# A down projection by seven multiplications: where the sums of weights are made

## The chip, the cores and the metric

The kernel runs on one core of a Trainium2 chip. The metric is the device time of one launch in microseconds; the kernel before was timed three times. All numbers of the profile are of one profiled execution on that core.

## What is computed

One decoder block on 256 tokens and 16 meta tokens, width 2048, in float32: a norm and one wide input projection, an RWKV-7 branch and a forgetting-attention branch side by side, a gated merge, an output projection, and a SwiGLU feed-forward network. Its last line is the part that is changed:

```python
def _layer(h, n1, w_in, ..., n2, w_gu, w_dn):
    ...
    h = h + merged @ w_o
    gate, up = jnp.split(_rms(h, n2) @ w_gu, 2, axis=-1)
    return h + (jax.nn.silu(gate) * up) @ w_dn
```

`w_dn` is 5632 x 2048. The result is held to float32 accuracy: every operand is split into a high part `wh` (rounded by ACT) and the rest `wl` (the difference, by DVE), and a product is three matmuls, high by high, high by low and low by high.

## The kernel before

The kernel is one program for five engines: PE (matmuls), ACT, DVE, POOL, and SP, which issues most DMAs. Weights are streamed once. A *job* is a slab of weights: a `load` (SP's DMA into one of four `raw` buffers, ACT's split into one of four `wh` buffers, DVE's into one of four `wl` buffers) and a `mul` (the matmuls). `run` issues the load of a job ahead of the matmuls of the job before it, so that splits run ahead of PE, by up to four buffers. `spawn` starts side work that is let in between by an estimate of PE's time, here the sums of activations (`sums_of_pairs`).

The down projection takes `w_dn` in 22 *pairs* of 128 rows (256 rows each) and two *column groups* `cg` of 1024 columns, each of two halves of 512. The activations of a pair, already split, are in `ach` and `acl`, 128 tokens by 128 rows a block, two blocks of tokens `t`. So a pair and a column group is a 2x2 product of blocks: activations A (tokens by rows) times weights B, with blocks b11, b12 (first 128 rows, left and right half) and b21, b22 (second 128 rows). There are two ways to do it:

- *slow* pairs (15 of 22): eight products, in two plain jobs of four products each, one for each half of the columns;
- *fast* pairs (7 of 22, `FAST`): seven products by Winograd's form of Strassen's scheme, with sums of blocks of A (made once, into `sst` and over a block of `acl` and `ach`) and sums of blocks of B, made for each column group. Four products (p1, p5, p6, p7) are added up over all fast pairs in four PSUM tiles `dnp` (`ps` in the code); the other three go straight into the plain accumulators `dn` (`cs`). After the last fast pair `sums_of_products` adds p1, p5, p6, p7 into the residual `hh` with one ACT copy (`u`) and eight additions on DVE.

A fast pair's sums of weights before: `load0` fetches b11, b12 in one DMA of 512 KB and b21, b22 in two of 256 KB, into two `raw` buffers; `load2` makes four differences on DVE, b12 - b11, b22 - (b12 - b11), b22 - b12 and b21 - (b22 - (b12 - b11)), into two `tt` tiles; splits of the raw blocks and of the differences feed the products, as four small jobs.

`ORDER` fixes which pairs follow each other: in column group 0 eight slow pairs, then fast and slow in turn; in column group 1 slow, fast, slow, slow, fast, and so on, with two slow pairs after the last fast one. The order of instructions within an engine is then set by the framework's own scheduler; each engine runs its instructions in that order, and waits at semaphores. The tiles `hts` (activations of the up projection) and `sst` share one buffer of the pool `hp`.

Of the kernel before, what the change touches and what calls it, by code (L numbers as in the profile page):

```python
# [18 lines left out]
P = 128  # L19
# [3 lines left out]
T = 256  # L23
# [18 lines left out]
for _n, _k in (("n1", 16), ("mu", 24), ("mu_w", 1), ("mu_a", 1), ("mu_g", 2), ("w0", 8), ("a0", 8), ("k_k", 8),  # L42
# [22 lines left out]
MIX = 0.47  # L65


FAST = [0, 1, 2, 3, 4, 5, 6]
# [48 lines left out]
def hybrid_block(ctx, tc, A, out, dbg=None):  # L117
# [391 lines left out]
    def split(hi, lo_, src):  # L509
        nc.scalar.activation(hi, src, AF.Copy)  # L510
        nc.vector.tensor_tensor(lo_, src, hi.bitcast(F32), op=ALU.subtract)
# [789 lines left out]
    hp = hp_pool.__enter__()  # L1301
    hh = hp.tile([P, 2, D], F32, tag="hh", name="hh")

    hts = hp.tile([P, KT, 2, L], F32R, tag="hts", name="hts")
# [32 lines left out]
    for j in range(4):  # L1337
        js = slice(j * 512, (j + 1) * 512)
        nc.sync.dma_start(hh[:, :, js], x[:, js].rearrange("(t p) c -> p t c", p=P))

        def post(t, ps, j=j, js=js):
            nc.vector.tensor_tensor(hh[:, t, js], ps, hh[:, t, js], op=ALU.add)
            jk = hp.tile([P, 512], F32, tag="jk", name=f"jk{j}{t}", bufs=2)
            nc.scalar.activation(jk, hh[:, t, js], AF.Square, accum_out=ss2[:, t, j:j + 1])
            if t == 0:
                return
            for k in range(4 * j, 4 * j + 4):
                pt = aux_ps(f"hT{k}")[:, :T]
                for t in range(2):
                    nc.tensor.transpose(pt[:, t * P:(t + 1) * P], hh[:, t, k * P:(k + 1) * P], ident)  # L1350
                tmp = hp.tile([P, T], F32, tag="htmp", name=f"htmp{k}", bufs=3)
# [63 lines left out]
    sst = sst[:, :len(fast) * 6 * P].rearrange("p (i s a c) -> p i s a c", i=len(fast), s=3, a=2)  # L1415

    def sums_of_pairs():

        at = 0
        for n in BATCHES:  # L1420
            fs, ps_ = slice(at, at + n), slice(fast[at], fast[at] + n)
            at += n
            h = lambda k, t: acp_h[:, ps_, k, t, :].bitcast(F32)
            l = lambda k, t: acp_l[:, ps_, k, t, :].bitcast(F32)
            f = [sst[:, fs, i, 1, :] for i in range(3)] + [acp_l[:, ps_, 0, 1, :]]
            hi = [sst[:, fs, i, 0, :] for i in range(3)] + [acp_h[:, ps_, 0, 1, :]]
            f32 = [hp.tile([P, T], F32, tag="ga", name=f"s{at}{i}", bufs=8)[:, :n * P].rearrange("p (i c) -> p i c", c=P)
                   for i in range(4)]
# [5 lines left out]
            tt(0, f32[0], l(1, 1), ALU.add)  # L1434
# [5 lines left out]
            tt(3, h(1, 0), f32[1], ALU.subtract)  # L1440
# [13 lines left out]
    def rows(ap):  # L1454
        return ap.rearrange("p (r c) -> p r c", c=T)

    def product(ps, a, w, half, first, last):
        o = ps.rearrange("p (a c) -> p a c", a=2)
        hi, lo_ = (x_[:, 2 * half:2 * half + 2] for x_ in w)
        nc.tensor.matmul(o, a[0], hi, start=first, stop=False)  # L1460
        nc.tensor.matmul(o, a[1], hi, start=False, stop=False)  # L1461
        nc.tensor.matmul(o, a[0], lo_, start=False, stop=last)  # L1462
        slot(3 * 512 / 2.4)

    def split_tiles():
        return [wp.tile([P, WCOLS], F32R, tag=t, name=t, bufs=WB).rearrange("p (r c) -> p r c", c=L)[:, :, s:s + T]
                for t, s in zip(("wh", "wl"), PLACE_T)]
# [17 lines left out]
            return load, mul  # L1485
        return [mk(0), mk(1)]

    def fast_jobs(i, cg, cs, ps, end):
        box = {}

        def b(k, x_):
            return wdn[i * 256 + k * P:i * 256 + (k + 1) * P, cg * 1024 + x_ * 512:cg * 1024 + (x_ + 1) * 512]

        def load0():
            ra, rb = (wp.tile([P, 1024], F32, tag="raw", name="raw", bufs=RAWB) for _ in range(2))
            nc.sync.dma_start(ra, wdn[i * 256:i * 256 + P, cg * 1024:(cg + 1) * 1024])
            for x_ in range(2):
                nc.sync.dma_start(rb[:, (1 - x_) * 512:(2 - x_) * 512], b(1, x_))
            box["r"] = rows(ra), rows(rb)
            w = split_tiles()  # L1500
            split(*(t[:, 0:2] for t in w), box["r"][0][:, 0:2])
            return w

        def load1():
            w = split_tiles()
            split(*w, box["r"][1])
            return w

        def load2():
            (b11, b12), (b22, b21) = ([r[:, 0:2], r[:, 2:4]] for r in box["r"])  # L1510
            w, v = split_tiles(), split_tiles()
            ts = [rows(hp.tile([P, 1024], F32, tag="tt", name="tt", bufs=2)) for _ in range(2)]
            t1, t2, t3, t4 = (t[:, 2 * n:2 * n + 2] for t in ts for n in range(2))
            for o, x_, y_ in ((t1, b12, b11), (t2, b22, t1), (t3, b22, b12), (t4, b21, t2)):
                nc.vector.tensor_tensor(o, x_, y_, op=ALU.subtract)
            split(*w, ts[0])
            box["v"] = v, ts[1]
            return w

        def load3():  # L1520
            v, t = box["v"]
            split(*v, t)
            return v

        first = i == fast[0]

        def mul0(w):
            if not ps:
                ps.extend(aux_ps(f"dnp{cg}{n}") for n in range(4))
            product(ps[0], a_of(i, 0, 0), w, 0, first, end)  # L1530

        def mul1(w):
            product(cs[1], s_of(i, 3), w, 0, False, False)
            product(cs[0], a_of(i, 1, 0), w, 1, False, False)

        def mul2(w):
            product(ps[1], s_of(i, 0), w, 0, first, end)
            product(ps[2], s_of(i, 1), w, 1, first, end)

        def mul3(w):  # L1540
            product(ps[3], s_of(i, 2), w, 0, first, end)
            product(cs[2], a_of(i, 1, 1), w, 1, False, False)
            if end:
                sums_of_products(cg, ps)
        return [(load0, mul0), (load1, mul1), (load2, mul2), (load3, mul3)]

    def sums_of_products(cg, ps):
        p1, p5, p6, p7 = ps
        h11, h12, h21, h22 = (hh[:, t, (2 * cg + x_) * 512:(2 * cg + x_ + 1) * 512] for t in range(2) for x_ in range(2))
        u = hp.tile([P, 512], F32, tag="jk", name=f"u{cg}", bufs=2)  # L1550
        nc.scalar.activation(u, p1, AF.Copy)
        for o, x_ in ((u, p6), (h11, p1), (h12, p5), (h12, u), (u, p7), (h22, p5), (h21, u), (h22, u)):
            nc.vector.tensor_tensor(o, x_, o, op=ALU.add)

    def post(cg, t, x_, ps):

# [7 lines left out]
    spawn(sums_of_pairs(), 2 * PAIRS)  # L1564
    for cg in range(2):
        cs, ps = [], []
        for i in ORDER[cg]:
            if i in fast:
                run(fast_jobs(i, cg, cs, ps, i == fast[-1]))
            else:  # L1570
                run(slow_jobs(i, cg, cs, i == ORDER[cg][-1]))
    finish_job()
    hp_pool.__exit__(None, None, None)
    ap_pool.__exit__(None, None, None)

# [60 lines left out]
```

## Time and profile before

| | |
|---|---|
| time of three runs | 1520.84 us median (1520.27 to 1521.56) |
| span of the profiled execution | 1517.7 us (its own time is given by the span alone) |
| busy share of PE, DVE, ACT, POOL | 99%, 73%, 53%, 7% |
| instructions of PE, DVE, ACT, POOL | 10071, 2009, 1230, 182 |
| granted TensorE clock, mean | 1.000 |
| bytes moved | 283.32 MB, 187 GB/s in the mean |
| down projection | about 1281 to 1518 us of the span |

The span is from the first to the last instruction; the time of a run holds some work around it. A row of a group reads: line, engine, operation, out<-in by tile names, shapes, count | busy us, mean ns of one | idle time of the engine before it, and what ended it. A row of waits reads: waiting engine and line <- releasing engine and line: us in all, times, longest. `SPq` and the like are an engine's DMA queue; "to landing" is from the issue of a DMA to the end of its data.

### The profile page before, as it was taken

To read this page: it belongs to the slowest core of one execution; us is meant where nothing else is said; L and a number is where in the kernel's file an instruction comes from. 1 tells how busy PE (TensorE), PEld (TensorE's weight loads), DVE (VectorE), ACT (ScalarE), POOL (GpSimd) and SP (SyncE) were. 2 spreads that over 40 slices of the span, in tenths; PEclk is the share of its full clock that TensorE was granted. 3 is DMA by queue.
4 is the path that set the end of the run, shared out by engine and by line. 5 is a ranking of instruction groups with operands and counts; after the bars stand their busy time and mean duration, and the time that the engine had idled before them with its cause. 6 is when DMAs were issued, how large, how long until landed. Compare 5 with 4: busy or idle time off the path is not lost.

```text
span 1517.7 us, 26174 instructions
## 1 busy us (share of the span) xinstructions
PE 1509.9 (99%) x10071; PEld 1339.5 (88%) x10071; DVE 1112.0 (73%) x2009; ACT 808.3 (53%) x1230; POOL 99.3 (7%) x182
## 2 busy tenths in 40 slices
PE   9999999999999999999999999999999999999998
PEld 9999999999989888998888888888888888887887
DVE  7888699689789857875665666566566658879776
ACT  7664565475465545644554555454455545554543
POOL 2112202202202000000000000000000000000000
PEclk9999999999999999999999999999999999999999
DMA  8557456646645757777566666666666666566664
GB/s 271 166 166 212 119 156 185 170 122 173 188 127 149 223 152 214 234 231 240 181 179 192 189 187 193 191 186 192 190 187 191 193 186 182 178 211 201 213 206 138
DMA packets 210365, 283.32 MB, mean 187 GB/s; under 512 B 24320, under 2 KB 129296, under 8 KB 210240
## 3 DMA queue, kind: packets, MB, share of 16 engines
q1 hardware_dynamic: 205344, 277.25, 61.9%
q10 hardware_dynamic: 4896, 4.40, 0.9%
q8 instruction: 79, 1.29, 0.3%
q14 instruction: 46, 0.38, 0.1%
HBM read 274.36 MB, written 7.24 MB: 186 GB/s over the span
## 4 chain that ended last, share of the span: by engine, by line
PE 95%; DVE 3%; DMA 1%; issue 1%; ACT 0%; SPq 0%; DVEq 0%; ACTq 0%
PE up L441 11%; PE gt L441 11%; PE zg L441 8%; PE gt L443 5%; PE up L443 5%; PE dn L1461 4%; PE dn L1460 4%; PE dn L1462 4%; PE zg L443 4%; PE f L441 2%; PE br L365 2%; PE br L366 2%; PE br L367 2%; PE f L365 2%; PE wo L1329 2%; PE wo L1331 2%
## 5 line engine op out<-in xcount | busy, mean ns | idle before, releaser
L336 DVE TENSOR_TENSOR wl<-raw,wh 128x1024 fp32r<-128x1024 f32 x460 | 561.9, 1226 | 281.3 <-ACT wh L335 280.6
L335 ACT ACTIVATE wh<-raw 128x1024 fp32r<-128x1024 f32 x460 | 486.5, 1059 | 470.2 <-PE up L441 118.9
L441 PE MATMUL gt<-hts,wh 128*128 128x512 f32 x704 | 242.9, 393 | 0.0
L441 PE MATMUL up<-hts,wh 128*128 128x512 f32 x704 | 242.7, 392 | 0.0
L443 PE MATMUL gt<-hts,wl 128*128 128x256 f32 x660 | 184.8, 280 | 0.0
L443 PE MATMUL up<-hts,wl 128*128 128x256 f32 x660 | 184.6, 280 | 0.0
L441 PE MATMUL zg<-xhl,wh 128*128 128x512 f32 x512 | 181.2, 399 | 0.0
L441 PEld LDWEIGHTS up<-hts,wh 128*128 128x128 f32 x704 | 130.0, 188 | 25.2
L441 PEld LDWEIGHTS gt<-hts,wh 128*128 128x128 f32 x704 | 129.9, 188 | 25.1
L443 PE MATMUL zg<-xhl,wl 128*128 128x256 f32 x480 | 134.3, 280 | 0.0
L443 PEld LDWEIGHTS up<-hts,wl 128*128 128x128 f32 x660 | 125.3, 190 | 1.8
L443 PEld LDWEIGHTS gt<-hts,wl 128*128 128x128 f32 x660 | 125.3, 190 | 1.8
L441 PEld LDWEIGHTS zg<-xhl,wh 128*128 128x128 f32 x512 | 94.3, 188 | 18.7 <-issue 0.7
L1460 PE MATMUL dn<-wh,ach 128*128 128x512 f32 x282 | 110.7, 393 | 0.0
L1461 PE MATMUL dn<-wh,acl 128*128 128x512 f32 x282 | 110.6, 392 | 0.0
L1462 PE MATMUL dn<-wl,ach 128*128 128x512 f32 x282 | 110.5, 393 | 0.0
L443 PEld LDWEIGHTS zg<-xhl,wl 128*128 128x128 f32 x480 | 90.9, 189 | 1.2
L365 PE MATMUL f<-xhl,wh 128*128 128x272 f32 x256 | 75.9, 296 | 0.0
L367 PE MATMUL f<-xhl,wl 128*128 128x272 f32 x256 | 73.6, 288 | 0.0
L366 PE MATMUL f<-xhl,wh 128*128 128x272 f32 x256 | 73.6, 288 | 0.0
L1462 PEld LDWEIGHTS dn<-wl,ach 128*128 128x128 f32 x282 | 52.9, 187 | 12.3 <-DVE wl L336 0.3
L1461 PEld LDWEIGHTS dn<-wh,acl 128*128 128x128 f32 x282 | 52.9, 188 | 12.0
(493 smaller groups left out, 3056.7 us busy)
## 6 DMA issues: line engine op xcount, KB each, us to landing
raw<-in_w_gate_up_dram SPq DMA_DIRECT2D x176, 512.0 KB, 4.3
raw<-in_w_in_dram SPq DMA_DIRECT2D x160, 512.0 KB, 3.9
raw<-in_w_down_dram SPq DMA_DIRECT2D x74, 512.0 KB, 5.0
raw<-in_w_o_dram SPq DMA_DIRECT2D x32, 512.0 KB, 4.3
raw<-in_w_branch_a_dram SPq DMA_DIRECT2D x16, 512.0 KB, 4.6
raw<-in_w_branch_b_dram SPq DMA_DIRECT2D x16, 512.0 KB, 5.0
raw<-in_w_down_dram SPq DMA_DIRECT2D x28, 256.0 KB, 4.6
zgd<-zg ACTq DMA_DIRECT2D x30, 128.0 KB, 3.8
```

The source lines that it names most:

```text
L335: nc.scalar.activation(th, rr, AF.Copy)
L336: nc.vector.tensor_tensor(tl, rr, th.bitcast(F32), op=ALU.subtract)
L365: nc.tensor.matmul(ps, wh, ah, start=first, stop=False)
L366: nc.tensor.matmul(ps, wh, al, start=False, stop=False)
L367: nc.tensor.matmul(ps, wl, ah, start=False, stop=last)
L441: nc.tensor.matmul(ps.rearrange("p (a t) -> p a t", a=2), wh, act, start=first, stop=last)
L443: nc.tensor.matmul(ps[:, :T], wl, act[:, 0, :], start=False, stop=False)
L1329: nc.tensor.matmul(o, ah[:, kt, ts_], hi, start=first, stop=False)
L1331: nc.tensor.matmul(o, ah[:, kt, ts_], lo_, start=False, stop=last)
L1460: nc.tensor.matmul(o, a[0], hi, start=first, stop=False)
L1461: nc.tensor.matmul(o, a[1], hi, start=False, stop=False)
L1462: nc.tensor.matmul(o, a[0], lo_, start=False, stop=last)
```

## The change

The differences of weights are no longer made by DVE from raw blocks. A fast pair has one *kept* tile `tt` of 128x1024 (five buffers, in a new pool `dn` that takes the place of `hts`), and the blocks are added into it by accumulating DMAs that POOL issues, one after the split of what stood there before:

| step | tile t, left and right half | split for | then |
|---|---|---|---|
| 0 | b11, b22 (two plain loads of 256 KB, ahead of time) | p1, and one product into `dn` | POOL: t += (b12, b12), 512 KB |
| 1 | b11 + b12, b22 + b12 | p5, p7 | POOL: left += b22, 256 KB; SP: right = b21 |
| 2 | b11 + b12 + b22, b21 | p6, and one into `dn` | POOL: left += b21, 256 KB |
| 3 | b11 + b12 + b22 + b21 | one into `dn` | |

Since only sums can be accumulated, signs are turned in the sums of activations (three of its ten operations) and in `sums_of_products`. The products are the same seven, in another order. The steps of several pairs are now interleaved: pairs go in groups of `TOGETHER` (three in column group 0, two in column group 1; the seventh pair, pair 6, is a group by itself in both), a group's steps in the order step 0 of each pair, step 1 of each pair, and so on. `EVERY` says how many plain jobs and how many steps take turns (1 and 2 in column group 0, 1 and 1 in column group 1), after `LEAD` plain jobs (12 and 2). The first loads of a pair's tile are issued up to `FETCH` = 4 steps ahead. At the end of a column group two plain jobs at least are kept back. The last up job is finished ahead of the change of pools, and `hts` and `htmp` live in a pool `ht` of their own.

```diff
-ORDER = [SLOW[:8] + [i for pair in zip(FAST, SLOW[8:]) for i in pair],
-         [i for n, f in enumerate(FAST) for i in (SLOW[2 * n], f, SLOW[2 * n + 1])] + SLOW[14:]]
+LEAD = (12, 2)
+EVERY = ((1, 2), (1, 1))
+TOGETHER = (3, 2)
+FETCH = 4
+KEPT = 5
...
-    sst = hp.tile([P, KT, 2, L], F32R, tag="hts", name="sst").rearrange("p k a t -> p (k a t)")
+    finish_job()
+    ht_pool.__exit__(None, None, None)
+    dn_pool = tc.tile_pool(name="dnp", bufs=1, reuse_waits="tile")
+    sst = dn.tile([P, len(fast), 3, 2, P], F32R, tag="sst", name="sst")
...
-            tt(0, h(0, 1), h(1, 1), ALU.add)
+            tt(0, h(0, 1), h(1, 1), ALU.subtract)
...
+        def halved(n):
+            t = box["t"]
+            w = split_tiles()
+            split(*(x_[:, :2 * n] for x_ in w), rows(t)[:, :2 * n])
+            return w
         def load0():
-            ra, rb = (wp.tile([P, 1024], F32, tag="raw", name="raw", bufs=RAWB) for _ in range(2))
-            nc.sync.dma_start(ra, wdn[i * 256:i * 256 + P, cg * 1024:(cg + 1) * 1024])
-            for x_ in range(2):
-                nc.sync.dma_start(rb[:, (1 - x_) * 512:(2 - x_) * 512], b(1, x_))
...
+            t = box["t"] = tile_of()
+            nc.sync.dma_start(t[:, :512], b(0, 0))
+            nc.sync.dma_start(t[:, 512:], b(1, 1))
+        def split0():
+            t = box["t"]
+            w = halved(2)
+            nc.gpsimd.dma_start(t.rearrange("p (x c) -> p x c", x=2),
+                                b(0, 1).unsqueeze(1).to_broadcast([P, 2, 512]), accum_op=ALU.add)
             return w
-        def load2():
...
-            for o, x_, y_ in ((t1, b12, b11), (t2, b22, t1), (t3, b22, b12), (t4, b21, t2)):
-                nc.vector.tensor_tensor(o, x_, y_, op=ALU.subtract)
+        def split1():
+            t = box["t"]
+            w = halved(2)
+            nc.gpsimd.dma_start(t[:, :512], b(1, 1), accum_op=ALU.add)
+            nc.sync.dma_start(t[:, 512:], b(1, 0))
             return w
+        def split2():
+            t = box["t"]
+            w = halved(2)
+            nc.gpsimd.dma_start(t[:, :512], b(1, 0), accum_op=ALU.add)
+            return w
+        def split3():
+            return halved(1)
...
         def mul0(w):
             product(ps[0], a_of(i, 0, 0), w, 0, first, end)
+            product(cs[1], s_of(i, 3), w, 1, False, False)
         def mul1(w):
+            product(ps[1], s_of(i, 0), w, 0, first, end)
+            product(ps[3], s_of(i, 2), w, 1, first, end)
+        def mul2(w):
+            product(ps[2], s_of(i, 1), w, 0, first, end)
             product(cs[0], a_of(i, 1, 0), w, 1, False, False)
         def mul3(w):
+            product(cs[2], a_of(i, 1, 1), w, 0, False, False)
             if end:
                 sums_of_products(cg, ps)
...
+        plain = [job for i in SLOW for job in slow_jobs(i, cg, cs, i == SLOW[-1])]
+        while at < len(FAST):
+            group = [fast_steps(i, cg, cs, ps, i == FAST[-1]) for i in FAST[at:at + TOGETHER[cg]]]
+            quick += [(load if n == 0 else None, steps[n]) for n in range(4) for load, steps in group]
+            at += TOGETHER[cg]
...
+        run(plain[:lead])
+        while n < len(quick):
+            ahead(min(n + max(FETCH, quick_n), len(quick)))
+            run([step for _, step in quick[n:n + quick_n]])
+            k = min(slow_n, len(plain) - 2)
+            run(plain[:k])
+        run(plain)
```

How it moves instructions is seen at the end of column group 0, at its last fast pair. In the rows below a name's number tells one buffer's use from another; `DMASW` is a DMA of POOL's queue, `DMAHW` one of SP's or ACT's.

ACT before, from the last fast pair's first split to the slow pairs' after it: the pair's splits (L510), one of a plain slab (L335), then the copy `u` of p1, and the next slabs.

```order
L510 ACTIVATE wh_15250<-raw_15245 128x2x256 [waits DMAHW3_49,DVE_49,PE_49]
L510 ACTIVATE wh_15266<-raw_15246 128x4x256 [waits DMAHW4_49,DMAHW5_49,DVE_49,PE_49]
L510 ACTIVATE wh_15273<-tt_15277 128x4x256 [waits DVE_49,PE_49,Activation_49]
L510 ACTIVATE wh_15275<-tt_15278 128x4x256 [waits DVE_49,PE_49,Activation_49]
L335 ACTIVATE wh_15300<-raw_15299 128x4x256 [waits DMAHW6_49,PE_49,Activation_49]
L1551 ACTIVATE u0_15311<-dnp00_14740 128x512 [waits PE_49]
L335 ACTIVATE wh_15322<-raw_15321 128x4x256 [waits DMAHW7_49,PE_49,Activation_49]
L335 ACTIVATE wh_15344<-raw_15343 128x4x256 [waits DMAHW0_49,DVE_49,PE_49]
L335 ACTIVATE wh_15366<-raw_15365 128x4x256 [waits DMAHW1_49,DVE_49,PE_49]
```

ACT after, the same place (line 513 is the old 510, 338 the old 335): pair 6's four splits of the one tile `tt_15124`, with the copy `u` behind the first, and plain slabs (`raw`) between.

```order
L513 ACTIVATE wh_15159<-tt_15124 128x4x256 [waits DVE_49,PE_49]
L1566 ACTIVATE u0_15236<-dnp00_14659 128x512 [waits PE_49]
L513 ACTIVATE wh_15176<-tt_15124 128x4x256 [waits DMASW2_49,DVE_49]
L338 ACTIVATE wh_15189<-raw_15188 128x4x256 [waits DMAHW3_49,DVE_49]
L513 ACTIVATE wh_15200<-tt_15124 128x4x256 [waits DMAHW5_49,DMASW3_49,DVE_49]
L513 ACTIVATE wh_15217<-tt_15124 128x2x256 [waits DMASW4_49,DVE_49,PE_49]
L338 ACTIVATE wh_15228<-raw_15227 128x4x256 [waits DMAHW4_49,DVE_49,PE_49]
```

The copy `u` of p1 stood behind all of the pair's splits and a plain one; now it stands ahead of the pair's second split, because p1 is complete with the first step. The second, third and fourth split each wait for a DMA of POOL's queue.

DVE before, there: a plain slab's split, then the sums of products into `hh` and `u`, with one plain split among them.

```order
L336 TENSOR_TENSOR wl_15301<-raw_15299,wh_15300 128x4x256 [waits DMAHW6_49,PE_49,Activation_49]
L1553 TENSOR_TENSOR hh_9122<-dnp00_14740,hh_9122 128x512 [waits Activation_49]
L1553 TENSOR_TENSOR u0_15311<-dnp02_14742,u0_15311 128x512 [waits PE_49]
L1553 TENSOR_TENSOR hh_9122<-dnp01_14741,hh_9122 128x512 x2
L1553 TENSOR_TENSOR hh_9122<-u0_15311,hh_9122 128x512 [waits DVE_49]
L336 TENSOR_TENSOR wl_15323<-raw_15321,wh_15322 128x4x256 [waits DMAHW7_49,Activation_49]
L1553 TENSOR_TENSOR u0_15311<-dnp03_14743,u0_15311 128x512 [waits DVE_49,PE_49]
L1561 TENSOR_TENSOR hh_9122<-dn00_14381,hh_9122 128x512 [waits PE_49]
L1553 TENSOR_TENSOR hh_9122<-u0_15311,hh_9122 128x512 [waits DVE_49]
```

DVE after, there: pair 6's splits (`wl` from `tt_15124`) and the sums of products, from the split of step 0 to the plain slab after step 3; the second additions of p5, u and p7 into `hh` that only repeat are left out.

```order
L514 TENSOR_TENSOR wl_15160<-tt_15124,wh_15159 128x4x256 [waits PE_49,Activation_49]
L1569 TENSOR_TENSOR hh_9122<-hh_9122,dnp00_14659 128x512 [waits Activation_49]
L514 TENSOR_TENSOR wl_15177<-tt_15124,wh_15176 128x4x256 [waits DMASW2_49,Activation_49]
L339 TENSOR_TENSOR wl_15190<-raw_15188,wh_15189 128x4x256 [waits DMAHW3_49,Activation_49]
L1569 TENSOR_TENSOR hh_9122<-hh_9122,dnp01_14660 128x512 [waits PE_49]
L514 TENSOR_TENSOR wl_15201<-tt_15124,wh_15200 128x4x256 [waits DMAHW5_49,DMASW3_49,Activation_49]
L1569 TENSOR_TENSOR u0_15236<-u0_15236,dnp02_14661 128x512 [waits PE_49]
L1569 TENSOR_TENSOR hh_9122<-hh_9122,u0_15236 128x512 [waits DVE_49]
L1569 TENSOR_TENSOR u0_15236<-u0_15236,dnp03_14662 128x512 [waits DVE_49]
L514 TENSOR_TENSOR wl_15218<-tt_15124,wh_15217 128x2x256 [waits DMASW4_49,Activation_49]
L339 TENSOR_TENSOR wl_15229<-raw_15227,wh_15228 128x4x256 [waits DMAHW4_49,Activation_49]
```

The sums of products stood behind the pair's last split; now each stands behind the step that completes its product, and five of them ahead of the split of step 3.

PE after, there: the last matmul of pair 6's step 0, then step 1 (`dnp01`, `dnp03` from `wh_15176`) with the plain job's (`wh_15189`) first matmuls among it.

```order
L1470 MATMUL dn01_14389<-wl_15160,ach_9877 128x512
L1468 MATMUL dnp01_14660<-wh_15176,sst_14375 128x512 [waits Activation_49]
L1469 MATMUL dnp01_14660<-wh_15176,sst_14375 128x512
L1468 MATMUL dnp03_14662<-wh_15176,sst_14375 128x512
L1469 MATMUL dnp03_14662<-wh_15176,sst_14375 128x512
L1468 MATMUL dn00_14388<-wh_15189,ach_9877 128x512 [waits Activation_49]
L1469 MATMUL dn00_14388<-wh_15189,acl_9878 128x512
L1470 MATMUL dnp01_14660<-wl_15177,sst_14375 128x512 [waits DVE_49]
L1470 MATMUL dnp03_14662<-wl_15177,sst_14375 128x512
L1468 MATMUL dn02_14390<-wh_15189,ach_9877 128x512
```

The high-part matmuls of the plain job stand ahead of step 1's low-part ones; step 1's own first matmuls follow directly on step 0. Before, a pair's four steps followed directly on each other too, but all its blocks had been loaded by then; now step 1 needs a split of the tile into which POOL's DMA adds after the split of step 0.

ACT after, at the end of column group 1, at its pair 6 (tile `tt_15987`): one plain slab after step 0 and one after step 1.

```order
L513 ACTIVATE wh_16069<-tt_15987 128x4x256 [waits DVE_49,PE_49]
L338 ACTIVATE wh_16087<-raw_16086 128x4x256 [waits DMAHW2_49,DVE_49,PE_49]
L513 ACTIVATE wh_16098<-tt_15987 128x4x256 [waits DMASW7_49,DVE_49,PE_49]
L338 ACTIVATE wh_16117<-raw_16116 128x4x256 [waits DMAHW3_49,DVE_49,PE_49]
L1566 ACTIVATE u1_16164<-dnp10_15395 128x512 [waits PE_49]
L513 ACTIVATE wh_16128<-tt_15987 128x4x256 [waits DMASW0_49,DMAHW6_49,DVE_49,PE_49]
L513 ACTIVATE wh_16145<-tt_15987 128x2x256 [waits DMASW1_49,DVE_49,PE_49]
L338 ACTIVATE wh_16156<-raw_16155 128x4x256 [waits DMAHW4_49,DVE_49,PE_49]
L338 ACTIVATE wh_16175<-raw_16174 128x4x256 [waits DMAHW5_49,DVE_49,PE_49]
```

Between the third and the fourth split nothing stands there; the last two plain slabs come behind the fourth.

More of the change, by code (lines that the diff above doesn't have):

```diff
@@ L1431, in tt @@
                 nc.vector.tensor_tensor(f32[i], x_, y_, op=op)
-            tt(0, h(0, 1), h(1, 1), ALU.add)
+            tt(0, h(0, 1), h(1, 1), ALU.subtract)
             tt(0, f32[0], l(0, 1), ALU.add)
-            tt(0, f32[0], l(1, 1), ALU.add)
+            tt(0, f32[0], l(1, 1), ALU.subtract)
             tt(1, f32[0], h(0, 0), ALU.subtract)
@@ L1439, in sums_of_pairs @@
             tt(2, f32[2], l(0, 1), ALU.subtract)
-            tt(3, h(1, 0), f32[1], ALU.subtract)
+            tt(3, f32[1], h(1, 0), ALU.add)
             tt(3, f32[3], l(1, 0), ALU.add)
@@ L1486, in slow_jobs, with fast_steps @@
         return [mk(0), mk(1)]
-    def fast_jobs(i, cg, cs, ps, end):
+    def fast_steps(i, cg, cs, ps, end):
+        first = i == fast[0]
         box = {}
@@ L1520, in load3, with tile_of @@
[L1520 to L1525, printed above, removed]
+        def tile_of():
+            return dn.tile([P, 1024], F32, tag="tt", name="tt", bufs=KEPT)
+        def halved(n):
[3 more added lines that the diff above has]
+            return w
+        def load0():
+            t = box["t"] = tile_of()
+            nc.sync.dma_start(t[:, :512], b(0, 0))
+            nc.sync.dma_start(t[:, 512:], b(1, 1))
@@ L1551, in sums_of_products @@
         nc.scalar.activation(u, p1, AF.Copy)
-        for o, x_ in ((u, p6), (h11, p1), (h12, p5), (h12, u), (u, p7), (h22, p5), (h21, u), (h22, u)):
-            nc.vector.tensor_tensor(o, x_, o, op=ALU.add)
+        for o, x_, op in ((u, p6, ALU.add), (h11, p1, ALU.add), (h12, p5, ALU.add), (h12, u, ALU.subtract),
+                          (u, p7, ALU.add), (h22, p5, ALU.add), (h21, u, ALU.add), (h22, u, ALU.subtract)):
+            nc.vector.tensor_tensor(o, o, x_, op=op)
     def post(cg, t, x_, ps):
@@ L1566, in hybrid_block, with ahead @@
         cs, ps = [], []
[L1567 to L1571, printed above, removed]
+        plain = [job for i in SLOW for job in slow_jobs(i, cg, cs, i == SLOW[-1])]
+        quick, at = [], 0
+        while at < len(FAST):
+            group = [fast_steps(i, cg, cs, ps, i == FAST[-1]) for i in FAST[at:at + TOGETHER[cg]]]
+            quick += [(load if n == 0 else None, steps[n]) for n in range(4) for load, steps in group]
+            at += TOGETHER[cg]
+        loads = [load for load, _ in quick]
+        lead, (slow_n, quick_n) = LEAD[cg], EVERY[cg]
+        def ahead(n):
+            for k in range(n):
+                if loads[k] is not None:
+                    loads[k]()
+                    loads[k] = None
+        run(plain[:lead])
+        del plain[:lead]
+        n = 0
+        while n < len(quick):
+            ahead(min(n + max(FETCH, quick_n), len(quick)))
+            run([step for _, step in quick[n:n + quick_n]])
+            n += quick_n
+            k = min(slow_n, len(plain) - 2)
+            run(plain[:k])
+            del plain[:k]
+        run(plain)
     finish_job()
+    dn_pool.__exit__(None, None, None)
     hp_pool.__exit__(None, None, None)
```

30 lines of the change are left out of this document (7 added, 23 removed).

## The prediction

> **What bounds the kernel now.** I read the page first (busy time, chain), then busy time by stretches of the down projection, the waits of PE, the groups of instructions by shape, and the DMA landings.
>
> ```profile
> span 1517.7 us, 26174 instructions
> ...
> PE 1509.9 (99%) x10071; PEld 1339.5 (88%) x10071; DVE 1112.0 (73%) x2009; ACT 808.3 (53%) x1230; POOL 99.3 (7%) x182
> ...
> PE 95%; DVE 3%; DMA 1%; issue 1%; ACT 0%; SPq 0%; DVEq 0%; ACTq 0%
> ```
>
> PE carries the chain; nothing else does for long. The stretches of the down projection, then PE's waits in it:
>
> ```profile
> core 0: us, PE busy (x) PEld busy (x) DVE busy (x) ACT busy (x) POOL busy (x), PEclk, DMA share, GB/s
> ...
> 1320.00:1390.00 70.00, 69.78 (x302) 56.25 (x301) 57.48 (x65) 40.30 (x42) 0.00 (x0) 1.00 0.60 189
> 1390.00:1440.00 50.00, 49.45 (x214) 39.59 (x213) 42.36 (x49) 24.37 (x25) 0.00 (x0) 1.00 0.67 217
> 1440.00:1480.00 40.00, 40.00 (x175) 32.59 (x174) 28.59 (x32) 18.57 (x20) 0.00 (x0) 1.00 0.64 204
> 1480.00:1514.00 34.00, 33.89 (x148) 27.26 (x146) 25.50 (x31) 13.75 (x15) 0.00 (x0) 1.00 0.42 138
> 1514.00:1518.00 4.00, 0.00 (x0) 0.00 (x0) 0.68 (x2) 0.00 (x0) 0.00 (x0) 1.00 0.36 119
> ```
>
> ```profile
> PE dnp L1460 <- ACT wh L510: 0.5, 1, 0.5
> PE dnp L1462 <- DVE wl L511: 0.2, 1, 0.2
> ```
>
> PE starts a 128x512 matmul every 40.00/175 = 0.229 us, as fast beside a DVE that is busy 0.71 of the time (1440 to 1480) as beside one at 0.85 (1390 to 1440). The change keeps every matmul: a plain job is 12 of them (2.74 us), a fast pair's four steps were 3, 6, 6 and 6 and are 6, 6, 6 and 3. So all there is to win is the idle time, 0.22 + 0.55 = 0.77 us; the last 3.8 us, after PE, are the same adds and stores. Whether the time moves is decided by new waits of PE.
>
> **The parts that cost nothing.**
>
> ```profile
> L1515 DVE TENSOR_TENSOR tt<-raw,tt 128x512 f32<-128x512 f32 x28 | 19.2, 686 | 11.5 <-DMA raw<-in_w_down_dram 11.4
> L1515 DVE TENSOR_TENSOR tt<-raw 128x512 f32<-128x512 f32 x28 | 19.2, 687 | 12.8 <-DMA raw<-in_w_down_dram 12.6
> ```
>
> DVE loses 56 subtractions, 38.4 us. PE did not wait for them beyond the 0.77 us, so they bring at most that. The sums of activations keep ten operations a batch: 0. The job finished ahead of the pools' change leaves ACT's and DVE's rows there in their old order: 0. SP issues 42 plain loads for the fast pairs before (3 a pair and column group) and 42 after; 42 accumulating ones are new on POOL, idle here. The first `tt` load on SP waits for the last up product, behind seven loads of plain slabs; the eighth slab's load waits for the fourth slab's split, which comes after that product too, so nothing is held up; gone wrong, it would delay one load (4.6 us) that plain jobs with three more slabs in hand cover.
>
> ```profile
> 700.43 0.97 SPq L1339 DMA_DIRECT2D hh<-in_x_dram  x2
> ```
>
> The four loads of `hh` move some 25 us earlier on SP, between the last branch loads. They wait for the last gate product, long done there, and take 0.97/2 us of SP each: with four `raw` buffers ahead 0, without that cover 1.9 us.
>
> **The part that costs: a chain through memory.** Before, a pair's three loads were all on their way at once. Now they form a chain: split t (ACT wh, DVE wl), accumulate into t, split again, three times. The durations:
>
> ```profile
> L335 ACT ACTIVATE wh<-raw 128x1024 fp32r<-128x1024 f32 x53 | 55.8, 1057 | 15.1 <-PE dn L1461 7.7 <-issue 4.7 <-PE dnp L1461 1.4
> L510 ACT ACTIVATE wh<-raw 128x512 fp32r<-128x512 f32 x14 | 8.9, 635 | 15.9 <-PE dn L1461 10.2 <-DMA raw<-in_w_down_dram 4.0 <-PE dnp L1461 1.7
> L1551 ACT ACTIVATE u<-dnp 128x512 f32<-128x512 f32 x2 | 1.2, 579 | 0.0
> L511 DVE TENSOR_TENSOR wl<-tt,wh 128x1024 fp32r<-128x1024 f32 x28 | 34.1, 1222 | 14.4 <-ACT wh L510 14.3
> L1553 DVE TENSOR_TENSOR hh<-dnp,hh 128x512 f32<-128x512 f32 x6 | 3.9, 680 | 0.0
> ```
>
> No accumulating DMA is in this trace. Nearest are the plain weight loads of the same sizes; here are issue to landing of the 256 KB halves (L1498), the 512 KB rows (L1496), the 512 KB slabs (L326), and the stores of 256 KB at the end:
>
> ```profile
> DMA to landing us min/median/max: 3.7/4.6/6.1
> ```
> ```profile
> DMA to landing us min/median/max: 4.7/5.0/5.3
> ```
> ```profile
> DMA to landing us min/median/max: 3.9/5.0/7.0
> ```
> ```profile
> out_dram<-hh SPq DMA_DIRECT2D x6, 256.0 KB, 2.4
> ```
>
> Call the time from a DVE split's end to the landing X1 (512 KB), X2 and X3 (256 KB). I take the medians 5.0, 4.6, 4.6 (sum 14.2): an accumulation must read its destination too, which adds, but it stands in POOL's empty queue, which takes off. Ends: 3.7 each (11.1; the b21 load must land for the third step anyway, and it is such a plain load) and 7.0 each (21.0). The store's 2.4 us is of an idle machine and a write, so no end.
>
> Where is it covered? Splits run at most four jobs ahead of PE (`wh` and `wl` have four buffers). In groups of three pairs (column group 0) step 3 of a pair comes, for the third pair, after one plain job and two fast steps; from its split's possible start to PE's need there are 10.95 us, and splits (1.06 + 1.22 + 0.64) take 2.9: covered up to X of 8.0. In groups of two with a plain job after each step, still more. But **pair 6 is alone in its group** in both column groups, with only one plain job, or none, between its steps.
>
> Column group 0, from the start of pair 4's last step on PE (there the buffer for pair 6 frees): PE wants step 0 at 0.69 + 0.69 + 2.74 = 4.11 and step 1 at 5.49. The split takes 2.35, so t lands at 2.35 + X1 = 7.35. ACT's next row is the copy u of p1, which waits for step 0's third matmul, 5.0, and ends at 5.55; only then split 1: it starts at 7.35, ends at 8.4. Wait 2.95 (if X1 were 0: 1.15). Steps 1 and the plain job take 4.25 on PE; after split 1's wl (1.2), X2 and split 2 (1.1) step 2 starts 6.9 after step 1: wait 2.7 and 0.3 for its wl. Step 2 ends 1.66 after its start, step 3's wh is there at 1.25 + 4.6 + 0.64 = 6.5: wait 4.85. The plain split stands behind split 3 on ACT: 0.6 more. Together 11.5, or X1 + X2 + X3 - 2.7. When X3 is small, DVE takes over: five sums of products (0.6 apart) stand ahead of split 3's wl.
>
> Column group 1 has a plain job between the first three steps. Counted in the same way PE wants step 2 at 14.4; it is ready at 2.35 + X1 + 2.3 + X2 + 1.1 = 15.3: wait 0.85, and 0.75 for wl. Step 3: 1.25 + 4.6 + 0.64 - 2.1 = 4.4. Plain split behind it: 0.6. Together 6.6, or the sum of X less 7.6.
>
> Sum: 11.5 + 6.6 = 18.1, less the 0.77 us of old waits: 17.3. Against its own execution 1517.7 becomes 1535.0; the median of the runs, 1520.84, lies 3.1 above that span, which I carry over: **1538 us**. With 3.7 each the waits are 8.4 + 3.6, so 1532; with 7.0 each 18.3 + 13.4, so 1552. With landings at once, u and the five sums alone would leave 4.4 + 1.6 us: 1526.
>
> The Trainium skill, page "DMA: Bandwidth & Descriptors", section "Anatomy of one DMA — SWDGE (gpsimd) path", fits a DMA issued by GpSimd as 2.0 us plus bytes over 436 GB/s, which for these sizes is 3.2 and 2.6 us by estimate. By that, with 3.7 for X2, the waits would be 6.8 + 2.4 and the time 1529 us; the trace has no such DMA to agree or differ.
>
> **Rivals.**
> - *Short landings.* POOL's queue is empty and engines are busy 0.60 to 0.67 of the time, so a landing could take 2.4 to 3.7 us: 1526 to 1532. Against it: none of the plain weight loads landed under 3.7 us. The fit above is such a case.
> - *Long landings.* A group of three pairs moves 8.65 MB in 30.9 us of PE, 280 GB/s, where 217 GB/s took a share of 0.67, that is 324 GB/s at full share. If the 3.1 MB that accumulate occupy the engines twice, it is 382 GB/s: the engines are full, the prefetched tiles only bridge it, landings go to 7 us or over, and groups may wait too: 1552 and more. The Trainium skill says on the same page, section "Issuing engines are not separate DMA queues", that DMAs of all issuing engines interleave on the same 16 engines; the trace shows only SP and ACT doing so.
> - *Not slower.* With less DVE work the old 0.77 us go, and the chain at pair 6 stays hidden because splits get further ahead than I count: 1520. It needs X1 under 2.0 us there and u out of the way; against it, ACT's order of rows is fixed and u waits for PE.
> - *The change does what it says* on DVE, but DVE is not what PE waits for.
>
> **Chances.** Forecast 0.52 (1532 to 1546), short landings 0.18, long 0.22, not slower 0.08. The range leaves out the last and the far end of the long case: 1527 to 1553. A measurement of this kernel tells about 0.2% (3 us) from no change. Faster by more needs more than PE's idle time: 0.02; within, 0.06; slower, 0.92.
>
> **What the changed profile would show.** PE's busy time and counts unchanged; DVE busy near 1074 us. PE idle in two places, at pair 6 of each column group, with ACT waiting there for `tt`; none inside the groups of three and two. POOL's 42 issues landing in 3.7 to 7 us. Idle PE spread over all groups would say long landings; PE idle under 6 us would say that I misread the splits' lead over PE. I am wrong if pair 6 does not hold the waits.

## Result and profile after

The changed kernel takes 1562.87 us (median of four runs, 1560.56 to 1565.48) against 1521.11 us for the kernel before (now four runs): a ratio of 1.0274, 95% interval 1.026 to 1.0289. The forecast was 1538 us, with a range to 1553: slower was right, by how much was not. The profiled execution's span is 1561.3 us, 43.6 more than before.

The page: PE's count is unchanged, and DVE lost 33.0 us of work.

```profile
span 1561.3 us, 26187 instructions
...
PE 1527.8 (98%) x10071; PEld 1345.3 (86%) x10071; DVE 1079.0 (69%) x1953; ACT 805.5 (52%) x1230; POOL 141.9 (9%) x224
```

PE has 17.9 us more of busy time for the same matmuls; that is our first sign that not only waiting was added. The waits of PE in the down projection (waiting engine and line <- releaser: us, times, longest):

```profile
PE dnp L1468 <- ACT wh L513: 13.3, 6, 5.6
PE dn L1468 <- ACT wh L513: 8.5, 2, 4.4
PE dnp L1470 <- DVE wl L514: 3.4, 8, 0.5
PE dn L1470 <- DVE wl L339: 1.1, 2, 0.5
```

26.3 us, where 0.77 stood before. By stretches (columns as in the prediction's table; the third row is pair 6 of column group 0, the fifth that of column group 1):

```profile
1281.00:1320.00 39.00, 39.00 (x171) 31.81 (x170) 34.43 (x68) 21.41 (x34) 4.70 (x4) 1.00 0.87 251
1320.00:1384.00 64.00, 59.83 (x242) 45.23 (x241) 32.71 (x30) 28.04 (x31) 14.34 (x15) 0.97 0.96 237
1384.00:1410.00 26.00, 15.64 (x42) 10.97 (x41) 14.24 (x16) 7.86 (x9) 1.76 (x2) 0.74 0.48 115
1410.00:1530.00 120.00, 116.44 (x494) 93.08 (x493) 62.16 (x57) 51.12 (x53) 18.97 (x19) 0.99 0.82 216
1530.00:1557.50 27.50, 19.09 (x64) 13.04 (x62) 13.79 (x19) 6.08 (x7) 1.77 (x2) 0.88 0.29 62
```

PE idles most at pair 6, but also in the groups ahead of it (4.2 and 3.6 us), and the DMA engines are busy 0.96 of the time in the groups of three. The chain of waits at pair 6 of column group 0 (start, us, what):

```profile
1380.34 1.23 DVE wl L514
1381.57 0.45 issue
1382.03 6.79 DMA tt<-in_w_down_dram
...
1388.90 1.07 ACT wh L513
1389.97 0.02 issue
1389.99 1.24 DVE wl L514
1391.23 0.36 issue
1391.58 4.59 DMA tt<-in_w_down_dram
...
1398.92 4.08 DMA tt<-in_w_down_dram
...
1403.11 0.64 ACT wh L513
```

This is the chain that the prediction described, link by link: split, accumulate, split. From the end of DVE's split to the landing it is 0.45 + 6.79 = 7.2 us, then 0.36 + 4.59 = 4.95. The third split by DVE ended at 1398.57, so the third link is 4.4.

PE's granted clock there, in steps of 2 us (PE busy with its instructions, PEclk, DMA share, GB/s):

```profile
1386.00:1388.00 2.00, 0.00 (x0) 1.00 0.60 101
1388.00:1390.00 2.00, 0.00 (x0) 0.74 0.04 6
1390.00:1392.00 2.00, 1.99 (x5) 0.50 0.00 0
1392.00:1394.00 2.00, 2.00 (x6) 0.50 0.67 160
1394.00:1396.00 2.00, 2.00 (x7) 0.56 0.98 242
1396.00:1398.00 2.00, 1.73 (x8) 1.00 0.32 123
```

After the 5.6 us gap PE works at half clock until about 1396: a matmul starts every 0.43 us.

Idle time alone therefore doesn't add up to 43.6 us. A better measure is lateness: the start of the n-th matmul of the down projection, less n times 0.2305 us (about PE's pace where it doesn't wait; n counts from 0) and less 1278.34 us, the start of the first one before. Worked out from PE's timeline, in us (zero matmuls not counted; differences in the text are of unrounded values):

| place | changed | plain, POOL | plain, SP | sums on DVE | zeros, 2 places | zeros, 3 places |
|---|---|---|---|---|---|---|
| first matmul | 0.7 | 0.9 | 0.2 | 1.2 | 0.2 | 0.3 |
| pair 6, group 0: step 0 | 9.1 | 1.4 | 0.4 | 2.9 | 9.5 | 8.5 |
| column group 1 | 25.8 | 16.1 | 10.6 | 3.3 | 24.8 | 25.1 |
| pair 6, group 1: step 0 | 32.5 | 16.2 | 10.9 | 3.6 | 31.0 | 33.4 |
| last matmul | 45.2 | 24.7 | 17.1 | 3.7 | 42.7 | 44.9 |

The kernel before ends at 1.7. So the changed one loses 8.4 us in the groups of column group 0, 16.7 at its pair 6, 6.6 in the groups of column group 1 and 12.7 at its pair 6. The other columns are experiments below.

### The profile page after: what moved, and what is told of

Same layout as the page of the kernel before. It is cut to its first block, busy times and chain, and to the rows that moved or that the text cites. A ratio compares the mean times of both kernels' runs of the same rounds, so it can differ in the third digit from the quotient of the medians.

```text
span 1561.3 us, 26187 instructions
## 1 busy us (share of the span) xinstructions
PE 1527.8 (98%) x10071; PEld 1345.3 (86%) x10071; DVE 1079.0 (69%) x1953; ACT 805.5 (52%) x1230; POOL 141.9 (9%) x224
## 4 chain that ended last, share of the span: by engine, by line
PE 87%; DMA 7%; DVE 2%; issue 2%; ACT 1%; POOL 0%; SPq 0%; DVEq 0%; ACTq 0%; POOLq 0%
PE gt L444 10%; PE up L444 10%; PE zg L444 8%; DMA tt<-in_w_down_dram 7%; PE gt L446 5%; PE up L446 5%; PE zg L446 4%; PE dn L1468 2%; PE dn L1469 2%; PE dn L1470 2%; PE f L444 2%; PE br L368 2%; PE br L369 2%; PE br L370 2%; PE f L368 2%
## 5 line engine op out<-in xcount | busy, mean ns | idle before, releaser
L514 DVE TENSOR_TENSOR wl<-tt,wh 128x1024 fp32r<-128x1024 f32 (+1 forms) x56 | 61.0, 1091 | 99.0 <-ACT wh L513 90.1
L1468 PE MATMUL dn<-wh,ach 128*128 128x512 f32 x282 | 115.3, 409 | 8.6 <-ACT wh L513 8.5
L513 ACT ACTIVATE wh<-tt 128x1024 fp32r<-128x1024 f32 (+1 forms) x56 | 53.2, 951 | 128.1 <-DMA tt<-in_w_down_dram 86.6
L1522 POOL DMA_DIRECT2D tt<-in_w_down_dram x14 | 17.2, 1227 | 849.9 <-DVE s L1439 771.6
L368 PE MATMUL f<-xhl,wh 128*128 128x272 f32 x256 | 75.8, 296 | 0.0
L1468 PEld LDWEIGHTS dn<-wh,ach 128*128 128x128 f32 x282 | 55.2, 196 | 23.6 <-ACT wh L513 10.3
```

The lines of the kernel that those rows point to most:

```text
L368: nc.tensor.matmul(ps, wh, ah, start=first, stop=False)
```

## Experiments

**Pair 6 no longer alone.**

```diff
-TOGETHER = (3, 2)
+TOGETHER = ((3, 4), (2, 2, 3))
```

> The seven fast pairs go in groups of three and four (column group 0) and of two, two and three (column group 1), so pair 6 is no longer alone; nothing else differs from the changed kernel. Theory A (the chain of landings at the lone pair 6, and the half clock that follows its waits, cost most): the 10.6 + 8.3 us of idle PE at pair 6, the restart of PE after each gap and some 8 us of half clock go, about 29 us in all, while the waits inside the other groups stay: 1533 us, 1528 to 1540. Rival B (the accumulating transfers fill the DMA engines, wherever they stand): pair 6's waits come back inside the larger groups: 1545 to 1562. Rival C (PE waits because splits run less far ahead with four steps in a row, not because of landings): no better than 1555.

1526.93 us, ratio to before 1.0037 (1.0026 to 1.0049). Its waits of PE:

```profile
PE dnp L1468 <- ACT wh L513: 2.0, 2, 1.3
PE dnp L1470 <- DVE wl L514: 1.6, 4, 0.5
PE dn L1470 <- DVE wl L339: 0.5, 1, 0.5
```

36 us come back from the grouping alone, more than A gave, although the 512 KB accumulation still lands late (a median of 10.8 us, against 8.7). Where other pairs' steps stand between, long landings are mostly hidden: the last matmul is 8.3 us late here. The groups lost less, too, which A had not expected: 8.1 us in all of them in place of 15.0 (the second group of column group 0, now of four pairs, 2.7 in place of 6.1). B and C fall as the main cause.

**The same transfers without accumulating.** Three calls lose their `accum_op` (two of them below), so this kernel leaves out the additions of weights and serves for its time alone:

```diff
-            nc.gpsimd.dma_start(t[:, :512], b(1, 1), accum_op=ALU.add)
+            nc.gpsimd.dma_start(t[:, :512], b(1, 1))
...
-            nc.gpsimd.dma_start(t[:, :512], b(1, 0), accum_op=ALU.add)
+            nc.gpsimd.dma_start(t[:, :512], b(1, 0))
```

> The three accumulating transfers of a pair become plain ones of the same size, on POOL's queue, over the same tile after the same splits; the additions of weights are left out. Order and waits stay. Theory B (reading the destination makes an accumulation occupy the DMA engines about twice as long): the share of POOL's queue in the down projection falls from 31.6% to about 16%, the 512 KB landing from 8.7 to 5 to 6 us, the 256 KB one from 5.6 to 4.5; the waits inside the groups (7.6 us idle, some 13 us with restart and half clock) go and pair 6 waits 6 us less: 1538 to 1547 us. Rival P (the issue by POOL is what is slow, some 1 us of descriptors and the start of its queue): landings stay at 8 and 5.5 us, 1556 to 1564. If theory A alone held (only the number of links counts), 1555.

1540.84 us, ratio 1.0124 (1.0107 to 1.0141), as B gave. The DMA rows of the down projection, of the changed kernel (queue: packets, MB, share of 16 engines; then issues: count, size, median us to landing):

```profile
q0 software_dynamic: 7840, 14.68, 31.6%
...
tt<-in_w_down_dram POOLq DMA_DIRECT2D x14, 512.0 KB, 8.7
tt<-in_w_down_dram POOLq DMA_DIRECT2D x28, 256.0 KB, 5.6
```

and of this one:

```profile
q0 software_dynamic: 4256, 14.68, 17.3%
...
tt<-in_w_down_dram POOLq DMA_DIRECT2D x14, 512.0 KB, 6.2
tt<-in_w_down_dram POOLq DMA_DIRECT2D x28, 256.0 KB, 4.2
```

For the same bytes an accumulation holds the engines 31.6/17.3 = 1.8 times as long, in 1.8 times as many packets. By the table, plain transfers lose 0.6 us in the groups in place of 15.0, and 23.1 at pair 6 in place of 29.4: the accumulation's own slowness was about 21 us, mostly in the groups. Whether the reading of the destination or the greater number of packets makes it slow wasn't separated.

**The same, issued by SP.** `nc.gpsimd` becomes `nc.sync` in the same three calls; the additions stay left out.

> As the run with plain transfers on POOL, but SP issues them (additions of weights left out). Theory: the path of the issue is worth 0.5 to 1 us a link, six links at pair 6, so 3 to 6 us under the plain transfers on POOL: 1534 to 1544 us, unless SP's queue, which now stands still until a split is done, delays the plain slabs behind it: then ACT waits for raw slabs and the time is 1550 to 1570. Rival P (POOL's path is the slow one): 1525 to 1533.

1535.95 us, ratio 1.0094 (1.0079 to 1.0109). Pair 6 loses 10.2 + 6.2 us in place of 14.7 + 8.5: the path by POOL costs 6.8 us over the six links, and PE's waits for plain slabs are 0.2 us, as with POOL: SP's queue delayed nothing that mattered. From the end of DVE's split to the start of ACT's next one, the six links take 24.0 us here, 28.8 plain by POOL and 34.2 accumulating: 0.8 us a link for POOL's path, 0.9 more for the adding. The first link of each column group, which holds X1, is 4.9 and 4.8 us here, 6.7 and 5.8 by POOL, 7.3 and 7.6 accumulating. What is left, 16.4 us, is the chain of plain transfers at the lone pair.

**Sums on DVE in the changed order.** Four blocks of a pair are loaded ahead into a kept tile (b12, b22, b11, b21):

```diff
+        def add(n, m):
+            nc.vector.tensor_tensor(block(n), block(n), block(m), op=ALU.add)
...
         def split0():
-            nc.gpsimd.dma_start(... b(0, 1) ..., accum_op=ALU.add)
+            w = halved(1, 2)
+            add(1, 0)
+            add(0, 2)
```

> Order, groups and steps of the changed kernel, pair 6 alone, but no accumulating transfer: the four blocks of a pair are loaded ahead by SP (1 MB, three kept tiles of four blocks) and DVE makes the four additions of 128x512 between the splits, as many DVE operations as the subtractions before. Theory A (the landings in the chain cost): a link is now one or two additions, 0.7 to 1.4 us, in place of 4.5 to 7.3 us, so only what the prediction called landings at once is left at pair 6, 4.4 + 1.6 us, and the group waits go: 1527 us, 1523 to 1531. Rival O (the order itself, four dependent steps in a row and the sums of products between them, costs): 1535 to 1550.

1520.52 us, ratio 1.0001 (0.9992 to 1.001): the time before, under A's 1523 to 1531, with 0.5 us lost at pair 6 where the prediction's floor was 6. Its chain there:

```profile
1373.57 1.24 DVE wl L514
1374.80 0.02 issue
1374.82 0.70 DVE tt L1517
1375.53 0.02 issue
1375.55 0.70 DVE tt L1517
...
1376.36 1.07 ACT wh L513
```

The link is 1.5 us in place of 7.2, with no landing and no semaphore of a queue in it. Four dependent steps at a lone pair, the interleaving and turned signs cost nothing: rival O falls. The row of `u` stands behind the third split in this kernel, ahead of the second in the changed one, so the floor from `u` wasn't tried as it was forecast.

**Sums on DVE, pair 6 grouped** (3, 2, 2 and 2, 2, 3).

> As the run with the additions on DVE, and pair 6 in a group with others: groups of 3, 2, 2 and of 2, 2, 3. Theory A: no wait of PE is left but tenths, 1520 to 1523 us, the time of the kernel before. Rival: DVE, with the subtractions' work again and the chain through it, makes PE wait in the small groups of column group 0: 1525 to 1532.

1520.06 us, ratio 0.9998 (0.9988 to 1.0007), as A gave. PE has one wait left in the down projection, of 0.9 us.

**Accumulating, groups of four and three in both column groups, six kept tiles.**

> The changed kernel with accumulating transfers, in groups of four and three in both column groups, six kept tiles. Between two steps of a pair more of PE's work stands than in the groups of 3, 4 and 2, 2, 3 (1526.9 us, 4.0 us of idle PE and 1.6 us of half clock). Theory A: covers landings of up to 11 us, so those waits go: 1521 to 1524 us. Rival B (the DMA engines are full, and a group of four asks for its accumulations in a bunch, so landings grow to 12 us and over): 1525 to 1532, no better than before it.

1525.03 us, ratio 1.0023 (1.0011 to 1.0034), 1.0 us over A's range and at the lower edge of B's, though no 512 KB accumulation took the 12 us of B (median 10.0, longest 11.7). One wait of 1.9 us and three smaller ones are left, all in column group 0, where the first groups' accumulations meet the fullest DMA engines (busy 0.97 of the time from 1281 to 1340 us, 0.92 to 1405). The best accumulating version still loses.

**Is the half clock a cause?** Zero matmuls are put into PE's gaps at pair 6, ahead of its steps 1 and 3:

```diff
         def mul1(w):
+            if end:
+                zeros(cs[1], (20, 9)[cg])
             product(ps[1], s_of(i, 0), w, 0, first, end)
...
         def mul3(w):
+            if end:
+                zeros(cs[1], 15)
             product(cs[2], a_of(i, 1, 1), w, 0, False, False)
```

> The changed kernel, with matmuls of a zero block added into a plain accumulator ahead of pair 6's step 1 (20 in column group 0, 9 in column group 1) and ahead of its step 3 (15 in both): 59 matmuls of 128x512, 13.5 us of work at full clock put into gaps of 5.6, 2.5, 4.4 and 4.0 us. Theory H (PE runs at half clock after a gap because it stood idle, for 3.4 us or twice that): the granted clock stays 1.00 at pair 6, some 8 us of slower matmuls and the slow restarts go: 1553 us, 1550 to 1558, although PE does more. Rival (the half clock comes from something else, the full DMA engines or the end of a column group): 1562 to 1568, with the clock at 0.5 in the same places.

1561.17 us (1560.25 to 1564.12), far above the 1553 of H. PE's timeline (start, us, instruction, what it waited for) shows the zeros and what came behind:

```profile
1384.65 4.82 PE L1432 MATMUL dn<-ach,zz 128*128 128x512 f32 x20
...
1397.64 0.80 PE L1477 MATMUL dnp<-wh,sst 128*128 128x512 f32 x1 [3.47 <-ACT wh L513]
```

The plain job behind step 1 ran at full clock and PE then stood 3.5 us before step 2, which started at 1397.64 where the changed kernel had 1397.36. The second run fills that gap too (18, 13 and 18 zero matmuls ahead of steps 1, 2 and 3 in column group 0; 8, 8 and 18 in column group 1):

> As the run with zero matmuls at pair 6, now ahead of three steps (18, 13, 18 in column group 0; 8, 8, 18 in column group 1), so that PE never idles there. The first such run kept the full clock in its first gap, and PE then waited 3.5 us at the next step instead: split 2 came at the same time. Theory H2 (half clock between two links of the chain is hidden by the chain; only that behind the last link costs, 13 + 9 slow matmuls of 0.196 us, and the slow restarts, 4.3 to 6 us in all): clock 1.00 at pair 6 and 1556 to 1559 us. Rival H (all half clock at pair 6 costs, 8 us, and the first run failed for its own gaps): 1551 to 1555. Rival N (the half clock costs nothing at all, the chain sets the end): 1561 to 1564.

1562.76 us (1561.81 to 1564.05), as N gave, with the full clock throughout at pair 6 of both column groups; the first part of column group 0's:

```profile
1388.00:1392.00 4.00, 1.96 (x8) 1.29 (x8) 2.46 (x3) 2.01 (x2) 0.86 (x1) 1.00 0.03 12
1392.00:1396.00 4.00, 4.00 (x19) 3.24 (x18) 1.10 (x2) 0.00 (x0) 0.04 (x1) 1.00 0.89 230
1396.00:1400.00 4.00, 3.08 (x12) 1.91 (x11) 1.22 (x1) 1.06 (x1) 0.23 (x1) 1.00 0.06 24
```

In the table pair 6 loses 16.6 + 11.5 us with the full clock against 16.7 + 12.7. The half clock adds to PE's busy time, but between two links PE only uses up time that it would have waited. Its own price at pair 6 is 1.3 us by this run and 2.4 by the first, and these figures are rough: in the first, step 3 started 1.3 and 1.0 us after its split, behind zeros that were still running, and in both the second link of column group 0 took 1.3 us longer than in the changed kernel, which wasn't followed up (the six links: 35.0 us in this run, 34.3 in the first, 34.2 in the changed kernel). In the groups, where no zeros were put, its price wasn't tried.

**Would a lighter DVE have been worth something?** The kernel before, with more fast pairs, spread evenly (`BATCHES`, `SLOW` and `ORDER` follow):

```diff
-FAST = [0, 1, 2, 3, 4, 5, 6]
+FAST = list(range(9))
```

> The kernel before (subtractions on DVE, loads ahead), with nine fast pairs in place of seven and a slow pair put between them where there is one. Two pairs less in plain form are 2 x 2 x 3 = 12 matmuls of 0.229 us less on PE, 2.75 us; DVE has some 9 us more in each column group. If PE alone bounds the down projection: 1517.8 us, 1516.8 to 1519. If DVE's room is smaller than its busy share says (the reason one could have for taking the sums from it): new waits for wl eat the gain, 1520 to 1526.

> The same with eleven fast pairs, half of all: 24 matmuls less, 5.5 us. DVE then has about 7.1 us a fast pair against PE's 4.8, 2.4 a slow pair against 5.5, so 104 us of splits and subtractions in 114 us of PE a column group, beside the sums of activations and of products. If PE alone bounds: 1515.3 us, 1514 to 1517. If DVE does: PE waits for wl in column group 0, where the sums of activations are, 1519 to 1530.

Nine: 1521.94 us, ratio 1.0007 (0.9998 to 1.0016), within the 1520 to 1526 us of new waits and not the 1517.8 of a PE that alone is the bound: the down projection has 3.8 us of waits for fast pairs' splits, and DVE is busy 38.6 of the 40 us from 1320 to 1360. Eleven: 1531.39 us, ratio 1.0068 (1.0055 to 1.0081). With eleven, in column group 0 (PE, PEld, DVE busy, ...):

```profile
1320.00:1360.00 40.00, 32.92 (x131) 24.47 (x130) 39.97 (x67) 20.44 (x28) 0.00 (x0) 0.96 0.46 151
```

DVE is busy 39.97 of 40 us there and PE 32.92. With seven fast pairs DVE has room; with nine it starts to be felt; with eleven it is the bound (the pairs' order changed with their number, so the point between is not exact). Less DVE work could pay only together with more fast pairs, by at most 1.4 us a pair (six matmuls), and the best accumulating version would need more than three further pairs to make up its 4.4 us. That combination wasn't tried, and no version here beats the kernel before.

## Why the prediction was wrong, and where it was right

- *Where it waits*: right. Idle PE at pair 6 is 10.3 and 8.3 us in the waits, against 11.5 and 6.6 forecast, and the runs with pair 6 grouped and with the sums on DVE confirm the mechanism. PE's waits at pair 6 of column group 0, then of column group 1 (one view for each):

```profile
PE dnp L1468 <- ACT wh L513: 5.9, 2, 5.6
PE dn L1468 <- ACT wh L513: 4.4, 1, 4.4
```
```profile
PE dn L1468 <- ACT wh L513: 4.0, 1, 4.0
PE dnp L1468 <- ACT wh L513: 3.5, 2, 2.5
PE dnp L1470 <- DVE wl L514: 0.8, 2, 0.5
```

  The agreement of the sums is luck. In column group 0 the steps 1, 2 and 3 waited 5.6, 0.3 and 4.4 us for `wh` where 2.95, 2.7 and 4.85 were forecast: PE at half clock used up most of the second (with the full clock, in the first run with zeros, it was 3.5). In column group 1 step 1 waited 2.5, where the prediction counted none, and steps 2 and 3 1.0 and 4.0, against 0.85 and 4.4. And in lateness these places cost 16.7 + 12.7 = 29.4 us, not 18.1.
- *The term X1, 5.0 us*: this failed first. "It stands in POOL's empty queue, which takes off" had the wrong sign. X1 measured 7.2 and 7.5 us, X2 4.95 and 4.9, X3 4.4 and 4.5. By the prediction's own formula that makes 13.9 + 9.3 = 23.2 us, 5.1 more than forecast; X2 and X3 were well sized. Plain transfers show the parts: issued by SP the first link is 4.9 and 4.8 us, near the 5.0 taken for X1; POOL's path adds 1.8 and 1.0, accumulating 0.6 and 1.8.
- *"Covered up to X of 8.0"*: this is the largest part of the miss. The landings passed the bound. For the second group of three the 512 KB accumulations landed so (the view of their line, for that stretch alone):

```profile
DMA to landing us min/median/max: 8.6/11.3/11.5
```

  PE's longest wait there, 1.8 us, was for the split behind the first of them, step 1 of the group's first pair. The groups lost 15.0 us where the forecast was none. Without accumulating they lost 0.6. This is the rival *long landings*, worked out as full engines at 382 GB/s and given 0.22: the row of share 0.67 for 217 GB/s was in hand, and the doubled bytes should have set X1 rather than the range's far end. That rival's signs, idle PE spread over the groups, are there.
- *"PE starts a matmul every 0.229 us"*: this was carried over to a PE that stands still. After the longer gaps it ran at half clock (a matmul every 0.43 us), and each gap costs some tenths beyond the idle time. Of 29.4 us at pair 6, 6.2 lie beyond the formula; some 1.3 to 2.4 of them are the half clock by the runs with zeros; what the rest is stays open (the slow starts behind gaps and the waits for `wl` weren't separated).
- *Short landings* of 2.4 to 3.7 us: refuted. The 512 KB accumulations measured 8.7, plain transfers of that size by POOL 6.2, the 256 KB ones 5.6 and 4.2 (medians). The fit of the Trainium skill, page "DMA: Bandwidth & Descriptors", section "Anatomy of one DMA — SWDGE (gpsimd) path", gives 3.2 us for 512 KB by estimate; the runs differ from it.
- *The floor of 4.4 + 1.6 us with landings at once*: not seen. With links of 1.5 us pair 6 lost 0.5, though in another order of ACT's rows.
- *Not slower*: refuted. *DVE isn't what PE waits for*: right; 33.0 us less DVE work bought nothing, and the changed order with the sums back on DVE is 42 us faster than with accumulating DMAs.
- *The parts at nothing*: the first down matmul came 0.7 us later than before, but 0.2 to 0.3 us in the four other accumulating kernels, which are the same up to there but for a block of zeros in two: no cost of the up and down projections' boundary or of the early `hh` loads is seen beyond what runs differ by.

Counted together: 0.7 at the start, 15.0 in the groups, 29.4 at pair 6 are 45.2 us; less the 1.7 of the kernel before, 43.5, the whole difference (lateness adds up by construction). The forecast had 18.1 at pair 6, nothing elsewhere, and 0.77 to take off, 17.3. So of the 26 us that the spans were missed by, 15.0 are the groups, 5.1 the mis-sized X1 at pair 6, and 6.2 what the formula there left out. The 3.1 us that the prediction carried over from span to run were too much: the profiled run of the changed kernel took 1.7 more than its span, so the runs were missed by 1.4 us less than the spans.

## What to carry to other kernels

A DMA that adds into a tile was a link of 4.4 to 7.5 us in a chain here, where a DVE addition was 0.7; try it in place of DVE work only where other work of PE stands between every two links, and look at the last, lone group of a loop, where that cover ends. Price such a transfer by the time that it holds the DMA engines, 1.8 times that of a plain one here, and ask whether they have that much room. When PE waits on a chain through other engines, count lateness, not idle time or clock: a slower PE between two links cost little here.

## What the runs showed of the hardware

In the groups of three one wait of 1.8 us was enough for the clock to fall (PE's busy time and clock, steps of 5 us):

```profile
1350.00:1355.00 5.00, 3.22 (x14) 0.98 1.04 228
1355.00:1360.00 5.00, 4.72 (x16) 0.68 1.04 205
```

At pair 6 of column group 1, waits of 1.0 and 0.5 us close together left it at 1.00, and half clock lasted 3.4 or 6.8 us. From the clocks of the 2 us steps, its changes lie at 1388.96, 1395.76, 1402.6, 1409.4, 1470.9, 1474.3, 1535.7, 1539.1, 1549.4 and 1552.8 us, all whole multiples of 3.41 us apart. The Trainium skill, page "TensorE: Matmul & The Clock Gate", section "Part 1: The HAM clock gate (the "warmup" mystery)", tells of a free-running window of 3413 ns, and the trace agrees. Counted on that grid, PE was busy 0.48 of the window from 1351.4 to 1354.8 us, behind which the clock fell, and 0.56 of the one from 1542.5 to 1546.0, with the two short waits, behind which it didn't. The Trainium skill's rule on the same page, in "HAM oscillation — how this bites in real kernels", no idle gaps over about 3.4 us, is too lenient here: 1.8 us, all within one window, was enough.
